# A streaming batch-norm kernel: GpSimd issues each store only after the store ahead of it has landed

## The chip, the cores and the metric

The kernel runs on one core of a Trainium2 chip. The metric is the device time of one execution in microseconds (us). Before the change three timed runs gave 2481.49, 2510.03 and 2502.17 us, so the median is 2502.17 us.

## The reference

The reference is a batch norm with given statistics over a tensor of 32 images, 256 channels and 128 x 128 pixels, all in float32. It is 537 MB in and 537 MB out.

```
eps = 1e-5
mean, var, gamma, beta: one value for each channel
return gamma * (x - mean) / np.sqrt(var + eps) + beta
```

Per channel this is one multiplication and one addition: `x * scale + shift` with `scale = gamma / sqrt(var + eps)` and `shift = beta - mean * scale`.

## The kernel before

The 256 channels are two blocks of 128, one channel per partition. An image's block is one tile of 128 partitions by 16384 floats: 8 MB, with 64 KB in each partition. There are 64 tiles (`NT = 64`), numbered i = 0 to 63, and three buffers (`NBUF = 3`), so tile i lives in buffer i % 3 and is changed in place.

Every tile passes through three steps:

- **Load.** SyncE issues the load of tile i on its own DMA queue. The first three loads are issued at once (L89 to L98; the first in two halves). From tile 3 on (L158 to L163) the load of tile i waits on the semaphore `stored[i % 3]`, which says that the store of tile i - 3 has landed, and so that the buffer is free.
- **Arithmetic.** ScalarE applies scale and shift to the whole tile in one instruction (L142), which waits for the load. VectorE takes part of the first and of the last tile (L131), and computes the scale and shift at the start.
- **Store.** GpSimd issues the stores of tiles 0 to 60 (L172), each of which waits for ScalarE (`adone`). ScalarE itself issues the last three (`NTAIL = 3`), on a queue of its own. GpSimd's stores add to `stored`, ScalarE's to `closed`.

A DMA is carried by 16 DMA engines. Each of them adds 1 to the DMA's semaphore when its share has landed, so a full landing is 16. With 128 partitions each engine carries 8 packets of 64 KB for a load and 8 for a store, and one completion packet of 4 bytes for each. The queues are q1 (SyncE's loads), q0 (GpSimd's stores) and q10 (ScalarE's last three stores).

The order is written out by hand, instruction by instruction on each engine. Nothing in it keeps GpSimd from issuing the store of tile i + 1 while the store of tile i is still under way. The loop that the change touches is the one at L165 to L174: it makes ScalarE's instruction of a tile and then the store of that tile.

Of the kernel before, what the change touches and what calls it, by code (L numbers as in the profile page):

```python
# [8 lines left out]
NBUF = 3  # L9
PAD = 936  # L10
NHEAD = 3
NTAIL = 3
# [5 lines left out]
def kernel(  # L18
# [18 lines left out]
    NT = N * NCB  # L37
# [25 lines left out]
    stored = [tc.alloc_semaphore(f"stored{s}") for s in range(NBUF)]  # L63
# [9 lines left out]
    with tc.tile_critical():  # L73
# [26 lines left out]
        def landed(i):  # L100
            if i < NHEAD:
                return first[i], 16
            s = i % NBUF
            before = 1 if s < NHEAD else 0
            return loaded[s], 16 * (i // NBUF + 1 - before)
# [34 lines left out]
        def scalar_part(i, first_col):  # L140
            t, cb = bufs[i % NBUF], i % NCB
            return nc.scalar.activation(  # L142
                out=t[:, first_col:],
                in_=t[:, first_col:],
                func=mybir.ActivationFunctionType.Identity,
                bias=shift_t[:, cb : cb + 1],
                scale=scale_t[:, cb : cb + 1],
            ).then_inc(adone, 1)


        def share(i):
            return VHEAD if i == 0 else VLAST if i == last else 0
# [12 lines left out]
        for i in range(NT):  # L165
            eng = nc.gpsimd if i < NT - NTAIL else nc.scalar
            packet = {"single_packet": True} if i < NT - NTAIL else {}
            written = (stored if i < NT - NTAIL else closed)[i % NBUF]
            scalar_part(i, share(i))._wait_ge(*landed(i))
            if i in (0, last):  # L170
                eng.wait_ge(vdone, 1 if i == 0 else 2)
            eng.dma_start(out=outr[i], in_=bufs[i % NBUF][:], **packet)._wait_ge(adone, i + 1).then_inc(  # L172
                written, 16
            )  # L174
# [39 lines left out]
```

## Time and profile before

| | us |
|---|---|
| median of the three timed runs | 2502.17 |
| profiled execution, its own time | 2481.47 |
| its span | 2479.7 |
| ScalarE busy | 885.6 |
| VectorE busy | 13.1 |
| GpSimd busy | 32.7 |
| one tile's arithmetic on ScalarE | 14.04 |
| step from one store's landing to the next, mean over stores 0 to 60 | 38.68 |
| first store: issue, landing on all engines | 31.00, 74.80 |
| last store of GpSimd (tile 60): issue, landing on all engines | 2346.87, 2395.83 |
| last store of all (tile 63): issue, landing on all engines | 2455.36, 2477.92 |

The profile is of one execution. Its page gives busy times for each engine, the share of time in which the 16 DMA engines moved something, the DMA queues, the time from issue to landing for each group of DMAs, and the chain of waits that ended last. Beneath the page lie the trace's records: each DMA packet with its start, duration, size and queue, and the time at which each DMA engine added its 1 to a semaphore. The landings in the table are read from these.

### The profile page before, as it was taken

The page shows a single profiled execution, that of the slowest core. Times are in us where ns is not written, and L with a number is a line of the kernel's source. Part 1 is how long each engine was busy: PE and PEld are TensorE (multiplying, and loading weights), DVE is VectorE, ACT ScalarE, POOL GpSimd, SP SyncE. Part 2 cuts the span into 40 slices and gives each one's busy share as a digit, 9 for nine tenths or more (in the row PEclk, how much of TensorE's full clock was granted, in tenths as well). Part 3 has the DMA queues.
Part 4 walks back from the last instruction along what each step waited for, and adds up shares of the span by engine and source line. Part 5 has one row for each costly group of instructions (what it writes and reads, how often), then busy time and mean ns, then how long its engine had stood idle before and what let it go on. Part 6 is the DMA issues. An engine that isn't in the chain of part 4 may idle for free.

```text
span 2479.7 us, 276 instructions
## 1 busy us (share of the span) xinstructions
DVE 13.1 (1%) x13; ACT 885.6 (36%) x66; POOL 32.7 (1%) x65
## 2 busy tenths in 40 slices
DVE  1000000000000000000000000000000000000000
ACT  2342432424424234242342433424334243342432
POOL 0000000000000000000000000000000000000000
DMA  9999999999999999999999999999999999999999
GB/s 410 437 440 426 437 440 428 434 440 432 430 440 432 430 440 433 429 440 436 427 440 436 427 440 437 426 440 437 426 440 437 426 440 438 425 440 438 425 440 406
DMA packets 18707, 1073.84 MB, mean 433 GB/s; under 512 B 2128, under 2 KB 2192, under 8 KB 2192
## 3 DMA queue, kind: packets, MB, share of 16 engines
q1 hardware_dynamic: 9488, 536.94, 50.0%
q0 software_dynamic: 8784, 511.71, 47.6%
q10 hardware_dynamic: 432, 25.17, 2.3%
q14 instruction: 3, 0.02, 0.0%
HBM read 536.94 MB, written 536.87 MB: 433 GB/s over the span
## 4 chain that ended last, share of the span: by engine, by line
another core or an unknown queue 61%; ACT 35%; DMA 2%; issue 0%; SPq 0%; DVE 0%; ACTq 0%; DVEq 0%
ACT t L142 35%; DMA t<-in_x_dram 2%; SPq L92 0%; DVE rows L90 0%; ACTq L172 0%; SPq L96 0%; DVE eps_t L108 0%; DVEq L209 0%; SPq L73 0%
## 5 line engine op out<-in xcount | busy, mean ns | idle before, releaser
L142 ACT ACTIVATE t<-t,shift_t,scale_t 128x16384 f32<-128x16384 f32 (+1 forms) x64 | 884.0, 13813 | 1554.8 <-DMA t<-in_x_dram 1554.8
L172 POOL DMA_DIRECT2D out_dram<-t x61 | 32.5, 534 | 2314.4 <-ACT t L142 2314.4
L131 DVE TENSOR_SCALAR t<-t,scale_t,shift_t 128x8192 f32<-128x8192 f32 (+1 forms) x2 | 9.6, 4812 | 2427.1 <-DMA t<-in_x_dram 2427.0
L115 ACT ACTIVATE std_t<-par,eps_t 128x2 f32<-128x2 f32 x1 | 0.3, 295 | 14.0 <-DVE par L113 14.0
L115 ACT ACT_TABLE_LOAD x1 | 1.3, 1283 | 0.9 <-SPq L73 0.9
L109 DVE STREAM_TRANSPOSE turned<-rows 32x1024 f32<-32x1024 f32 x1 | 1.2, 1233 | 11.9 <-DMA rows<-in_running_mean_dram 11.9
L90 DVE MEMSET rows<- 32x1024 f32 x1 | 0.9, 912 | 1.2 <-SPq L73 1.2
L113 DVE COPY par<-turned 32x8 f32<-32x8 f32 x4 | 0.6, 162 | 0.1
L122 DVE RECIPROCAL rstd_t<-std_t 128x2 f32<-128x2 f32 x1 | 0.2, 166 | 0.4 <-ACT std_t L115 0.4
L124 DVE TENSOR_TENSOR ms_t<-par,scale_t 128x2 f32<-128x2 f32 x1 | 0.2, 163 | 0.0
L125 DVE TENSOR_TENSOR shift_t<-par,ms_t 128x2 f32<-128x2 f32 x1 | 0.2, 161 | 0.0
L123 DVE TENSOR_TENSOR scale_t<-par,rstd_t 128x2 f32<-128x2 f32 x1 | 0.2, 160 | 0.0
L198 POOL MEMSET const-float32-0.0<- 128x1 f32 x1 | 0.1, 98 | 0.2 <-issue 0.2
L198 POOL MEMSET const-bfloat16-1.0<- 128x1 bf16 x1 | 0.1, 101 | 0.0
L198 POOL MEMSET const-float32-1.0<- 128x1 f32 x1 | 0.1, 98 | 0.0
L198 POOL MEMSET const-uint8-127<- 128x1 uint8 x1 | 0.1, 98 | 0.0
L108 DVE MEMSET eps_t<- 128x1 f32 x1 | 0.1, 59 | 0.1
## 6 DMA issues: line engine op xcount, KB each, us to landing
t<-in_x_dram SPq DMA_DIRECT2D x2, 4096.0 KB, 15.9
t<-in_x_dram SPq DMA_DIRECT2D x63, 55.3
out_dram<-t POOLq DMA_DIRECT2D x61, 46.2
out_dram<-t ACTq DMA_DIRECT2D x3, 32.2
rows<-in_running_var_dram SPq DMA_DIRECT2D x1, 16.0 KB, 11.3
rows<-in_gamma_dram SPq DMA_DIRECT2D x1, 16.0 KB, 11.1
rows<-in_beta_dram SPq DMA_DIRECT2D x1, 16.0 KB, 10.8
rows<-in_running_mean_dram SPq DMA_DIRECT2D x1, 16.0 KB, 10.7
```

The costliest lines, as they stand in the source:

```text
L90: zeroed = step(nc.vector.memset(rows[:], 0.0))
L109: step(nc.vector.transpose(out=turned[:], in_=rows[:]), fetched, 16 * NPAR)
L113: placed = step(nc.vector.tensor_copy(out=flat[q * B : (q + 1) * B], in_=blocks[:, :, q, 0]))
L115: nc.scalar.activation(out=std_t[:], in_=var_t, func=mybir.ActivationFunctionType.Sqrt, bias=eps_t[:], scale=1.0,)._wait_ge(vec, placed).t ...
L122: step(nc.vector.reciprocal(out=rstd_t[:], in_=std_t[:]), act, 1)
L123: step(nc.vector.tensor_mul(out=scale_t[:], in0=gamma_t, in1=rstd_t[:]))
L124: step(nc.vector.tensor_mul(out=ms_t[:], in0=mean_t, in1=scale_t[:]))
L125: ready = step(nc.vector.tensor_sub(out=shift_t[:], in0=beta_t, in1=ms_t[:]))
L131: return nc.vector.tensor_scalar(out=t[:, first_col:end], in0=t[:, first_col:end], scalar1=scale_t[:, cb : cb + 1], scalar2=shift_t[:, cb ...
L142: return nc.scalar.activation(out=t[:, first_col:], in_=t[:, first_col:], func=mybir.ActivationFunctionType.Identity, bias=shift_t[:, cb : ...
L172: eng.dma_start(out=outr[i], in_=bufs[i % NBUF][:], **packet)._wait_ge(adone, i + 1).then_inc(written, 16)
L198: nc = _bacc.Bacc("TRN2", target_bir_lowering=False, num_devices=1)
```

## The change

Two lines are added to the loop over tiles. For tiles 1 to 61, ahead of the tile's arithmetic and store, the engine that is to issue the store waits until the semaphore of the store before has its full 16 for that store.

```diff
         for i in range(NT):
             eng = nc.gpsimd if i < NT - NTAIL else nc.scalar
             packet = {"single_packet": True} if i < NT - NTAIL else {}
+            if i and i <= NT - NTAIL:
+                eng.wait_ge(stored[(i - 1) % NBUF], 16 * ((i - 1) // NBUF + 1))
             written = (stored if i < NT - NTAIL else closed)[i % NBUF]
             scalar_part(i, share(i))._wait_ge(*landed(i))
             if i in (0, last):
                 eng.wait_ge(vdone, 1 if i == 0 else 2)
             eng.dma_start(out=outr[i], in_=bufs[i % NBUF][:], **packet)._wait_ge(adone, i + 1).then_inc(
                 written, 16
             )
```

For tiles 1 to 60 the waiting engine is GpSimd. For tile 61 it is ScalarE, and there the wait stands ahead of tile 61's arithmetic as well, because both are ScalarE's. No DMA, no arithmetic and no buffer is added or taken away, and the loads' own waits stay as they were.

## The prediction

> **What bounds the kernel now.** I read the page from the DMA rows down, since ScalarE, the busiest engine, works only 36% of the span.
>
> ```profile
> DMA  9999999999999999999999999999999999999999
> ...
> DMA packets 18707, 1073.84 MB, mean 433 GB/s; under 512 B 2128, under 2 KB 2192, under 8 KB 2192
> ## 3 DMA queue, kind: packets, MB, share of 16 engines
> q1 hardware_dynamic: 9488, 536.94, 50.0%
> q0 software_dynamic: 8784, 511.71, 47.6%
> q10 hardware_dynamic: 432, 25.17, 2.3%
> ```
>
> The three shares add to 99.9%: the 16 DMA engines are busy for the whole span, so DMA time is the bound, and any idle time of the DMA engines is added to the end. The packet records say it more sharply. A 64 KB packet lasts 2.418 us, the starts of an engine's packets are mostly 2.414 us apart, and no engine is without a packet for more than about 1 us in all between its first and its last. A tile costs an engine 8 load and 8 store packets, 16 x 2.415 = 38.64 us; the landings of the stores are 38.68 us apart on average. The engines take a packet from q0 and one from q1 in turn.
>
> Next, the DMA issues, what SyncE's queue waits for, and the timeline of one tile:
>
> ```profile
> t<-in_x_dram SPq DMA_DIRECT2D x63, 55.3
> out_dram<-t POOLq DMA_DIRECT2D x61, 46.2
> ```
>
> ```profile
> SPq L160 <- DMA out_dram<-t: 2369.7, 61, 69.4
> ```
>
> ```profile
> 902.91 14.04 ACT L142 ACTIVATE t<-t,shift_t,scale_t 128x16384 f32<-128x16384 f32 x1 [24.59 <-DMA t<-in_x_dram]
> 917.25 0.53 POOL L172 DMA_DIRECT2D out_dram<-t  x1 [38.10 <-ACT t L142]
> 924.84 38.93 SPq L160 DMA_DIRECT2D t<-in_x_dram  x2
> 941.56 14.04 ACT L142 ACTIVATE t<-t,shift_t,scale_t 128x16384 f32<-128x16384 f32 x1 [24.61 <-DMA t<-in_x_dram]
> 955.89 0.53 POOL L172 DMA_DIRECT2D out_dram<-t  x1 [38.12 <-ACT t L142]
> ```
>
> A store needs 46.2 us and the next is issued after 38.6, so stores overlap: one is issued at 917.25, the one ahead of it lands at 924.82, which releases the load at 924.84. For 7.6 us of each tile two stores are queued. Also, the load before that one lands only at 941.5, 16.7 us after the store: when a store lands, an engine still has three to four load packets in hand. Both queues always hold something, which is why no engine stops.
>
> ```profile
> 924.80:941.50 16.70, 0.00 (x0) 0.00 (x0) 0.00 (x0) 1.00 1.01 440
> ```
>
> This window (fields before the last three: engines' busy times and the clock; then DMA share and GB/s) is the stretch between that landing and the load's: full rate.
>
> **The change part by part.** *The wait itself.* It binds: ScalarE has the next tile ready 7.6 us before the store ahead lands. Behind it on GpSimd are later stores only. The instruction costs GpSimd nothing that counts (32.7 us busy of 2479.7).
>
> *What it does to the queues.* In each tile an engine has 8 new load packets and 8 new store packets. While the store runs they alternate, so 8 stores take 7 or 8 loads along. But the next store now has to be asked for after the landing, and until it arrives the engine takes loads alone. The only row of a store arriving with none under way is the first: issue 31.00, first q0 packets at 35.2 to 38.2, so 4.2 us and up to one or two load packets. That is 9 to 10 loads per tile against 8 new ones: the three to four packets in hand are used up within about four tiles. From then on no load is left when a store lands, and the next load cannot be on its way, since its buffer is the one that the store has just freed. Load and store are then both asked for in the same moment, and the DMA engines stand still until the first load packet.
>
> *The size of that stop.* From the end of an engine's last store packet to its next load packet:
> - Completion to landing. The slowest engine's completion packet of store 0 starts at 74.46 and the landing is at 74.80: 0.34 us. The very last store has 2477.59 to 2477.92: 0.33. I take 0.34.
> - SyncE's reaction: landing 74.80, issue 74.82: 0.02 us.
> - Issue to data. The row that shows it with idle engines is the kernel's first load: issued at 0.96, first packet records from 1.96 on, first packets of 32 KB ended at 3.79 to 4.18. Such packets later take 1.21, so the work began in effect at 2.58 to 2.97, 1.6 to 2.0 us after the issue. The next store waits for the slowest engine, so I take 2.0; the lower end is 1.0, issue to first record.
>
> Together 2.36 us a tile, with a lower end of 1.36.
>
> *The store's own arrival* (4.2 us or more after the landing) is covered by the new load, whose 8 packets are 19.3 us of work; without that cover it would add 2.2 us a tile.
>
> *A stretch on arrival.* As store 0 joined, load packets at 32 to 38 us took up to 3.2 us in place of 2.42; per engine the excess is 0.3 to 1.0, mean 0.70. Once per tile this would now recur, if it belongs to a store that meets pure loads; it would not, if it belongs to the first use of q0 (that issue took 0.67 us, later ones 0.53). One row cannot tell, so I take half, 0.35, and keep 0 and 1.0 as ends.
>
> *Start and tail.* With loads still in hand after store 0, the first tiles wait for the store's arrival rather than for a load, some 2.4 us (one packet) more in sum. At tile 61 ScalarE waits for store 60 before its arithmetic; store 61 is then issued 14.4 us after that landing, beside load 63 with 19.3 us of packets, so the engines stay busy. After store 60's landing there remain 32 packets of an engine (load 63, stores 61 to 63): 77.3 + 2.0 + 0.3 = 79.6 us, against 82.1 now (2395.83 to 2477.92), where part of load 62 was still to come. The two nearly cancel: nothing.
>
> *Sum.* 2.36 + 0.35 = 2.71 us for each of 60 steps from store to store, 163 us. On the profiled execution, 2481.5 + 163 = 2644. The median of the runs shown is 20.7 above that execution and the lowest run equals it, so I add half, 10: 2655. Low: 60 x 1.36 = 82, 2563. High: 60 x (2.36 + 1.0) = 202 and 20.7 for the median, 2704, plus a few us for an engine's hiccup (0.34 us gaps occur) that the other 15 now wait for.
>
> *A rule beside the completion row.* The Trainium skill, page "DMA: Bandwidth & Descriptors", section "Anatomy of one DMA — SWDGE (gpsimd) path", puts a fixed cost of some 2.0 us on such a DMA, most of it the receipt of the write by the target memory. By it the stop would be 2.0 in place of 0.34, an estimate of 100 us more, 2755. The trace's 0.34 and 0.33 speak against it here.
>
> **The rivals.**
> 1. *Load packets in hand still cover the stop: no change, 2482 to 2502.* The place is the store's landing, the point one load packet in hand on every engine, 2.41 us against a stop of 2.36. For: today 16.7 us of loads are in hand there. Against: the 8 to 8 count; a load asked for at one landing finishes ahead of or with the store that it alternates with. It needs the store to be served more often than the load. 0.07.
> 2. *GpSimd's issue becomes the bound.* If loads stay in hand all the same while each store arrives late, a tile is completion behind one load packet 2.41 + 0.36 + 4.2 + 15 packets 36.2 = 43.2, up to 4.6 more than now: 60 x 4.6 = 276, 2758 to 2780. Against: loads would run ahead and run out. 0.04.
> 3. *A slow receipt that is hidden now.* Today a load packet runs between an engine's last store packet (ended 72.05 on the slowest) and its completion packet (74.46), so up to 2.41 us of receipt could be hidden. With none left to run there it would show: 2.71 + 2.41 = 5.12 a tile, 307, 2790 to 2810. Against: the last store, with no packet between, landed 0.33 after its last packet. The page cited above states such a receipt. 0.03.
> 4. *Faster, as fewer stores mix.* The duration of a packet would have to fall; it is 2.418 with loads alone (22.8 to 32) and with the two in turn. 0.02.
> 5. *The wait changes nothing*, or *the whole 46.2 us becomes the step* (60 x 7.5 = 450, 2930): the first is excluded by the 7.6 us, the second by the fact that 46.2 holds the wait behind the other store. Together 0.01, to slower.
>
> **How the numbers follow.** The stop forecast has 0.83, and its bounds 2563 to 2710 carry nearly all of that, so the range is 2560 to 2710. Slower by over 1% (25 us, which is what the three runs' own spread allows to be told): 0.83 + 0.04 + 0.03 + 0.01 = 0.91. Within 1%: 0.07. Faster: 0.02.
>
> **What would show it.** The GB/s row should fall from 433 to about 405 evenly from the second or third slice on, with the DMA share at 9 tenths or just under. Store issue to landing should fall from 46.2 to about 41, store issues should stand within 1 us behind SyncE's load issues, and the load's landing time should fall from 55.3 to about 38, since it waits behind no other load. GpSimd's waits should pass from ScalarE to the store's landing. Each packet should stay at 2.42 and a gap of 2 to 3 us appear on all 16 engines once a tile. I am wrong if packets lie in q1 at a landing (rival 1 or 2) or if a gap is over 4 us (rival 3).

## The result, and the profile after

The changed kernel took 2720.3 us (median of five runs, 2717.74 to 2725.26) against 2508.97 for the kernel before in five runs (2481.49 to 2513.75). The ratio is 1.0895, 95% interval 1.084 to 1.0951: slower, as forecast, but 65 us above the forecast and 10 us beyond its range. The profiled execution is the one of 2720.3 us; its span is 2718.5, 238.8 longer than before.

The page's DMA rows after the change. The first is GB/s in 40 equal slices of the span, the others are the queues with their share of 16 engines' span:

```profile
GB/s 418 415 357 386 401 398 389 401 386 401 401 386 401 386 401 401 386 401 386 401 401 386 401 386 401 400 378 409 371 417 386 386 414 376 414 385 387 408 394 401
...
q1 hardware_dynamic: 9488, 536.94, 49.4%
q0 software_dynamic: 8784, 511.71, 43.5%
q10 hardware_dynamic: 432, 25.17, 2.1%
```

The rate falls from 433 to 395 GB/s on average, evenly but for the third slice, which holds one long step (see below), and a few late ones. The shares now add to 95.0%, where they added to 99.9%: for one twentieth of the span the DMA engines have no packet. That q1's share hardly fell although the span grew says that its packets became longer.

The DMA issues (median us to landing):

```profile
t<-in_x_dram SPq DMA_DIRECT2D x63, 39.9
out_dram<-t POOLq DMA_DIRECT2D x61, 41.8
```

What GpSimd waits for (us in total, times, longest), first before the change, then after it, and then ScalarE after it:

```profile
POOL out_dram L172 <- ACT t L142: 2314.4, 61, 38.3
```

```profile
POOL out_dram L174 <- DMA out_dram<-t: 2531.2, 60, 52.7
ACT t L142 <- DMA t<-in_x_dram: 1696.5, 61, 36.5
```

A load lands 39.9 us after its issue, not 55.3: it no longer waits behind another load. GpSimd waited 2314 us for ScalarE before; now it waits 2531 us for stores to land.

One tile in the timeline, and three windows of it (start:end, length, busy times of three engines, clock, DMA share, GB/s):

```profile
932.15 14.04 ACT L142 ACTIVATE t<-t,shift_t,scale_t 128x16384 f32<-128x16384 f32 x1 [28.66 <-DMA t<-in_x_dram]
934.55 85.00 SPq L160 DMA_DIRECT2D t<-in_x_dram  x3
935.08 0.53 POOL L174 DMA_DIRECT2D out_dram<-t  x1 [42.17 <-DMA out_dram<-t]
```

```profile
934.20:935.50 1.30, 0.00 (x0) 1.30 (x1) 0.42 (x1) 1.00 0.00 0
935.50:976.60 41.10, 0.00 (x0) 12.93 (x2) 0.11 (x1) 1.00 0.98 408
976.60:977.70 1.10, 0.00 (x0) 1.10 (x1) 0.42 (x1) 1.00 0.00 0
```

ScalarE gets its tile at 932.15, so the load had landed by then and nothing is left in q1. The store lands at 934.54, SyncE asks for the load at 934.55, GpSimd for the next store at 935.08. No packet starts on any engine until after 935.5, and the same gap follows a tile later.

The packet records show how the growth divides. Over the execution a DMA engine stood without a packet for 137.1 us on average (0.6 before), and its packets were 102.9 us longer in all than at 2.42 us each (0.6 before). Standing and packets together fill the span, so their growth, 136.5 + 102.3 = 238.8 us, must be the growth of the span; what the records add is the share of each. For each of 60 steps between landings that is 2.28 us of standing and 1.70 us of longer packets, 3.98 us.

### The profile page after: what moved, and what is told of

The parts are those of the page before. It is cut to its first block, busy times and chain, and to the rows that moved or that the text cites. A ratio compares the mean times of both kernels' runs of the same rounds, so it can differ in the third digit from the quotient of the medians.

```text
span 2718.5 us, 337 instructions
## 1 busy us (share of the span) xinstructions
DVE 13.1 (0%) x13; ACT 885.6 (33%) x66; POOL 32.7 (1%) x65
## 4 chain that ended last, share of the span: by engine, by line
DMA 93%; another core or an unknown queue 2%; ACT 2%; issue 1%; SPq 0%; POOLq 0%; DVE 0%; ACTq 0%; POOL 0%; DVEq 0%
DMA out_dram<-t 93%; ACT t L142 2%; DMA t<-in_x_dram 1%; SPq L92 0%; POOLq L169 0%; DVE rows L90 0%; ACTq L174 0%; POOL out_dram L174 0%; DVE eps_t L108 0%; DVEq L211 0%; ACTq L169 0%; SPq L73 0%; POOLq L180 0%
## 6 DMA issues: line engine op xcount, KB each, us to landing
t<-in_x_dram SPq DMA_DIRECT2D x2, 4096.0 KB, 15.8
t<-in_x_dram SPq DMA_DIRECT2D x63, 39.9
```

## The experiments

The theory after the result was that of the prediction: the 16 DMA engines stop because, when a store lands, no load packet is in hand, no store is queued, and both are asked for only then. The rivals were a cost of GpSimd's way of issuing, a cost of serialised stores as such, and too few buffers. In all runs every tile is computed; `after` below means the changed kernel. Ratios are against runs of the kernel before on the same chip.

### Two stores may overlap again

```diff
-            if i and i <= NT - NTAIL:
-                eng.wait_ge(stored[(i - 1) % NBUF], 16 * ((i - 1) // NBUF + 1))
+            if i > 1 and i <= NT - NTAIL + 1:
+                eng.wait_ge(stored[(i - 2) % NBUF], 16 * ((i - 2) // NBUF + 1))
```

> GpSimd waits for the landing of the store two tiles back instead of one. Theory (the cost is the stop of all DMA engines when a store lands with no load packet in hand and no store queued): the store two back has landed some 31 us before the tile is ready, so two stores may still overlap, the wait never binds, and the time is that of the kernel before, 2481 to 2514 us, with stores landing 38.6 to 38.7 us apart. Rival (a wait of GpSimd for a store's semaphore costs something itself, whichever store it names): some part of the 4.0 us a tile stays, 2530 us or more.

Measured 2492.41 us against 2482.09, ratio 1.0023 (0.9977 to 1.0069); stores land 38.68 us apart in its trace, and GpSimd waits for ScalarE as before the change, for no landing:

```profile
POOL out_dram L174 <- ACT t L142: 2314.4, 61, 38.5
```

A wait that does not bind costs nothing that can be measured. This run does not tell whether the missing load or the missing store behind the landing costs the time; the halves below do.

### A store issued 10 us later

```diff
                 eng.wait_ge(stored[(i - 1) % NBUF], 16 * ((i - 1) // NBUF + 1))
+                if eng is nc.gpsimd:
+                    for _ in range(10):
+                        inst = nc.gpsimd.memset(pad[:], 0.0)
+                        if padded[0]:
+                            inst._wait_ge(slow, padded[0])
+                        inst.then_inc(slow, 1)
+                        padded[0] += 1
```

> As the changed kernel, but GpSimd also fills a scratch tile ten times (about 10 us) between the store's landing and the issue of the next store. Theory (the new load's 8 packets, 19.3 us of work, cover the store's arrival): the time stays within 1% of the changed kernel, 2695 to 2750 us, and store issue stands some 10 us after the load's issue. If the stretch of the second load packet belongs to the store's arrival, it moves to the packets that run then and the second one lasts 2.4 us; if it belongs to loads that start on idle engines, packets one and two stay at 3.2 and 3.4 us. Rival (GpSimd's issue is on the path): 60 x 10 = 600 us more, about 3300 us.

Measured 2718.01 us in one run. Its timeline:

```profile
929.71 0.33 SPq L162 DMA_DIRECT2D t<-in_x_dram  x1
929.81 9.30 POOL L174 MEMSET pad<- 128x936 f32 x10 [32.84 <-DMA out_dram<-t]
939.06 0.53 POOL L183 DMA_DIRECT2D out_dram<-t  x1
```

The store goes out 9.4 us after the landing instead of 0.5, and the time is that of the changed kernel: the load covers the store's arrival, and GpSimd's issue is not on the path. Where the longer packets went is read from one DMA engine's packets after a landing (us after it : duration, L from the load's queue, S from the store's). The records do not name the engine; a chain is put together from packets that start where another ends:

```
after       1.09:3.23 L  4.31:3.31 L  7.62:2.42 S 10.04:2.42 L 12.45:2.42 S
late_store  0.98:3.23 L  4.20:2.42 L  6.61:2.42 L  9.03:2.43 L 11.45:3.44 L 14.89:2.42 S
```

The first packet is long in both, by 0.67 us on average: that is the load's start on an idle engine. The other long one is no longer the second packet but the last load packet ahead of the first store packet, by 0.95 us on average after the change and 1.26 here. It belongs to the store's arrival. That the two totals agree to 2 us has some luck in it: the median step is 42.58 us here against 42.29, but one long step of the changed kernel (53.27 us, see below) is missing.

### A store issued 23 us later

The edit is the same with `range(25)`.

> As the run with ten fills ahead of GpSimd's store, with 25 fills, 23.2 us by the 0.93 us of one fill there. Theory (a load's 8 packets end some 21 us after the landing and cover a store that arrives before that): the store now arrives about 27 us after the landing, the engines stand a second time for 5 to 7 us, the stretch at the arrival goes because no load runs then, and the tile is about 47 us: 2950 to 3050 us. Rival (a late store costs nothing, or all of its lateness): 2718 us, or 23 x 60 = 1390 us more.

Measured 2824.95 us in one run: the estimate was too high, though the second stop and the missing stretch are there. Four windows of one tile:

```profile
920.40:921.40 1.00, 0.00 (x0) 0.00 (x0) 0.83 (x1) 1.00 0.00 0
921.40:941.80 20.40, 0.00 (x0) 0.00 (x0) 19.13 (x23) 1.00 0.98 411
941.80:944.90 3.10, 0.00 (x0) 2.52 (x1) 2.48 (x4) 1.00 0.00 0
944.90:964.90 20.00, 0.00 (x0) 11.52 (x1) 0.00 (x0) 1.00 0.97 419
```

Loads alone, then 3.1 us without a packet, then stores alone. GpSimd issued the store at 943.86 and the packets start at 945.0, 1.1 to 1.2 us later, not 4.2. So a store of GpSimd reaches an idle engine about as soon as a load does (1.0 us and more); on an engine at work with loads it waits for the packet that runs and for one more. A tile takes 44.4 us here, and no packet ahead of a store is long: with no load running there is no stretch.

### ScalarE issues the stores

```diff
-            eng = nc.gpsimd if i < NT - NTAIL else nc.scalar
-            packet = {"single_packet": True} if i < NT - NTAIL else {}
-            if i and i <= NT - NTAIL:
-                eng.wait_ge(stored[(i - 1) % NBUF], 16 * ((i - 1) // NBUF + 1))
+            eng = nc.scalar
+            packet = {}
             written = (stored if i < NT - NTAIL else closed)[i % NBUF]
             scalar_part(i, share(i))._wait_ge(*landed(i))
+            if i and i <= NT - NTAIL:
+                eng.wait_ge(stored[(i - 1) % NBUF], 16 * ((i - 1) // NBUF + 1))
```

> ScalarE issues all stores on its own queue, each after the landing of the one ahead (the wait stands behind the tile's arithmetic); GpSimd issues none. Theory (the stop is common to any queue, since load and store are asked for at the same landing): 2.0 us of standing and 0.7 us of start remain, 2640 to 2680 us if the stretch at the store's arrival is a matter of GpSimd's queue, 2690 to 2730 us if any store brings it. Rival (the cost is GpSimd's way of issuing): 2481 to 2520 us.

Measured 3221.24 us in one run, far above every expectation. Timeline and one window:

```profile
930.54 51.39 SPq L160 DMA_DIRECT2D t<-in_x_dram  x2
930.60 0.34 ACTq L174 DMA_DIRECT2D out_dram<-t  x1
```

```profile
930.60:981.60 51.00, 0.00 (x0) 14.04 (x1) 0.00 (x0) 1.00 0.89 329
```

Load and store are issued 0.06 us apart, and a tile takes 51 us: an engine stands 357 us in the whole run and its packets are 384 us longer, about half of them over 2.6 us, all through the tile. The shares of one store land 5.7 us apart at the median. Two runs look for the cause. The first takes the wait away, with all stores still ScalarE's:

> ScalarE issues all stores, each right behind its tile's arithmetic, with no wait for the store ahead: the control for the run with serialised stores on ScalarE's queue, whose tile took 51 us with packets of up to 3.4 us. If ScalarE's queue beside SyncE's is slow by itself, stretched packets appear here too and the time is 2600 us or more; if the stretching needs load and store to arrive together on idle engines, packets are 2.42 us and the time is 2480 to 2520 us.

Measured 2503.66 us, packets 15.5 us longer in all: ScalarE's queue beside SyncE's is not slow by itself. The second keeps the wait but lets eight fills by GpSimd pass between the landing and ScalarE's issue:

```diff
             if i and i <= NT - NTAIL:
-                eng.wait_ge(stored[(i - 1) % NBUF], 16 * ((i - 1) // NBUF + 1))
+                for n in range(8):
+                    inst = nc.gpsimd.memset(pad[:], 0.0)
+                    if n == 0:
+                        inst._wait_ge(stored[(i - 1) % NBUF], 16 * ((i - 1) // NBUF + 1))
...
+                eng.wait_ge(slow, padded[0])
```

> As the run with serialised stores on ScalarE's queue (51 us a tile), but between the landing and the store's issue GpSimd fills a scratch tile eight times, some 7.4 us, and ScalarE waits for that; the load goes out at once. If the stretched packets of that run came from load and store reaching idle engines together, the tile falls to 41 to 43 us and the time to 2630 to 2740 us. If they come from two hardware queues that restart at each landing, whatever their order, the tile stays at 50 us or more, 3150 us or more.

Measured 2710.0 us, with this timeline:

```profile
927.13 43.33 SPq L162 DMA_DIRECT2D t<-in_x_dram  x2
927.16 7.42 POOL L174 MEMSET pad<- 128x936 f32 x8 [35.22 <-DMA out_dram<-t]
934.67 0.34 ACTq L184 DMA_DIRECT2D out_dram<-t  x1
```

A later store makes the kernel 511 us faster. On these two queues the disorder of the serialised run needs load and store to reach idle engines together. With a few load packets ahead, ScalarE's store costs what GpSimd's costs, and the packet ahead of the store is as long here (3.3 to 4.1 us in the tile shown): the stretch is not GpSimd's. Why packets stay long for a whole tile after a common start is not settled.

### Halves: a load in hand at the landing

```diff
-            inst = nc.sync.dma_start(out=bufs[s][:], in_=xr[i])
-            if i >= NBUF:
-                inst._wait_ge(stored[s], 16 * (i // NBUF))
-            inst.then_inc(loaded[s], 16)
+            for half, sem in ((left, stored), (right, stored2)):
+                inst = nc.sync.dma_start(out=bufs[s][:, half], in_=xr[i][:, half])
+                if i >= NBUF:
+                    inst._wait_ge(sem[s], 16 * (i // NBUF))
+                inst.then_inc(loaded[s], 16)
...
                 eng.wait_ge(stored[(i - 1) % NBUF], 16 * ((i - 1) // NBUF + 1))
+                eng.wait_ge(stored2[(i - 1) % NBUF], 16 * ((i - 1) // NBUF + 1))
...
+            for half, sem in ((left, stored), (right, stored2)):
+                eng.dma_start(out=outr[i][:, half], in_=bufs[i % NBUF][:, half], **packet)._wait_ge(
+                    adone, i + 1
+                ).then_inc(sem[i % NBUF], 16)
```

> Loads and GpSimd's stores move a tile as two halves of 4 MB. Both halves of a store still wait until both halves of the store ahead have landed; a half's load waits only for that half's store, so it is asked for while the other half is still being stored. Theory (the cost is that load and next store are asked for at the same landing, with no load packet in hand): a half load is now in hand when the store lands, so the standing of about 2 us and the start of 0.8 us go and only the stretch at the store's arrival, about 1 us, is left: 2500 to 2620 us. Rival (serialising GpSimd's stores costs by itself): 2690 us or more.

Measured 2564.01 us against 2498.34, ratio 1.0273 (1.0196 to 1.035). The control has the halves without the wait:

> The same halves without the wait for the store ahead: the control for the run before. Both theories: the DMA engines stay full, 2480 to 2520 us.

Measured 2510.39 us in one run. The DMA issues of the run with the wait:

```profile
t<-in_x_dram SPq DMA_DIRECT2D x124, 4096.0 KB, 21.9
out_dram<-t POOLq DMA_DIRECT2D x122, 4096.0 KB, 35.2
```

GpSimd's stores are serialised as strictly as in the changed kernel, tile by tile. Yet an engine now stands only 6.4 us in the whole run instead of 137.1: when the second half of a store lands, 15.8 of the 16 engines are in the middle of a load packet on average. The longer packets remain, 68.5 us against 16.6 in the control, 0.87 a tile. This is the theory's central test: with load packets in hand the standing goes and the stretch stays, although the next store is still asked for only after the landing.

### Half-size tiles in six buffers

```diff
-NBUF = 3
+NBUF = 6
-NTAIL = 3
+NTAIL = 6
...
-    HW = H * W
-    NT = N * NCB
+    HW = H * W // 2
+    NT = N * NCB * 2
```

> Tiles of half the size (4 MB, 128 of them) in six buffers that take the same space, with the wait for the store ahead (the last six stores are ScalarE's, without it). Theory (each landing costs the same, since loads run ahead and then every buffer is loaded and waits, so the next load can again be asked for only at the landing): 3.7 to 4.0 us at each of 121 landings, 2930 to 2990 us. Rival (three buffers are too few; with six some load is always in hand): 2480 to 2620 us.

Measured 2863.09 us, ratio 1.1476 (1.1334 to 1.1619). The control:

> The same six half-size buffers without the wait: the control. Both theories: 2480 to 2520 us.

Measured 2487.65 us in one run. With the wait, load and store are again asked for half a microsecond apart at the landing:

```profile
911.88 45.30 SPq L162 DMA_DIRECT2D t<-in_x_dram  x3
912.40 0.53 POOL L176 DMA_DIRECT2D out_dram<-t  x1 [22.01 <-DMA out_dram<-t]
```

More buffers in the same space do not help: a landing costs (2861.1 - 2485.9) / 121 = 3.1 us by the spans of the two profiled executions, though a tile has half the bytes, so the cost goes with the number of landings. It is less than the 3.7 to 4.0 expected: by the packet records 1.8 us of standing and 1.4 us of longer packets, which at 32 KB are shorter by themselves.

### The wait at every fourth tile

```diff
-            if i and i <= NT - NTAIL:
+            if i and i % 4 == 0 and i <= NT - NTAIL:
```

> The wait stands only at every fourth tile, 15 waits instead of 61. Theory: load packets in hand (three to four an engine when a store lands) cover one late store, and the following free stores restore them, so the engines stand still hardly at all; what is left is the stretch of two load packets when a store arrives, about 1 us a wait: 2485 to 2530 us. Rival (each serialised landing costs its 4.0 us on its own, whatever lies in hand): 15 x 4.0 = 60 us, 2545 to 2575 us.

Measured 2597.09 us, ratio 1.0426 (1.0359 to 1.0494). Both sides missed: 15 waits cost 115 us by the medians and 112 by the spans of the profiled executions, over 7 each, more than a wait in the changed kernel. Windows around the landing at 516.0, for which GpSimd waits:

```profile
468.00:507.00 39.00, 0.00 (x0) 14.04 (x1) 0.00 (x0) 1.00 1.03 447
507.00:516.00 9.00, 0.00 (x0) 0.00 (x0) 0.00 (x0) 1.00 0.22 95
516.00:517.00 1.00, 0.00 (x0) 0.00 (x0) 0.46 (x1) 1.00 0.76 262
```

For 9 us ahead of the landing most engines have nothing to do; the semaphore's records show the first engine's share landing 16.3 us before the last one's. At the first two waited landings it is 3.1 and 2.3 us, at the later ones mostly 14 to 16. The spread is 3.1 us at the median in the kernel before and 0.78 in the changed kernel, where all engines restart together at each tile. With three free tiles between two waits, one to three of the 16 engines come to lag. The others end 5 to 7 us ahead of the waited landing, and "landed on all engines" means waiting for the few. What makes them fall behind stays open. A run in which GpSimd waits for one engine's share of the store ahead instead of all 16 (2680 to 2725 us expected, 2480 to 2600 if the wait for the last engine is what costs) gave no result, because such a wait can pass before the store has landed; so a wait for fewer engines is untested.

## Why the forecast was wrong in size

- **What bounds the kernel: right.** The growth lies in the DMA engines, 136.5 us of standing and 102.3 of longer packets, and GpSimd's issue is off the path: 9.4 us after the landing instead of 0.5, it leaves the time as it is.
- **Loads run out, and load and store are asked for at the same landing: right.** Nothing is in q1 at the landing, GpSimd's issue is 0.53 us behind SyncE's, and the first step, with loads still in hand, is 43.29 us against the 43.2 worked out. Halves put a load in hand and the standing goes.
- **The size of the stop: too small, and with no end above it.** It was 2.36 us a tile, which was also its highest value. The measured counterpart is 2.28 us of standing and 0.67 of the load's first packet, 2.95. The single terms were right for the slowest engine: 0.36 us from its last packet's end to the landing, and first load packets 1.0 us and more after the issue. What was left out is that every other engine waits for the slowest one. On average an engine ends its last packet 1.02 us ahead of the landing (the long step below left aside), and its first load packet starts 1.2 us after it. The steps of 43 us among the typical 42.3 are, after the first, those in which the shares of a store land 1.5 to 2.0 us apart.
- **The stretch on arrival: off by most.** Half of 0.70 us was taken because one row could not tell a first use of the queue from a store that meets running loads. Taking the store later moved the long packet along with it, giving it no load to meet removed it, and ScalarE's queue shows it too. It recurs at every landing, 0.95 us in the changed kernel; with a few more long packets it is 1.70 - 0.67 = 1.03 against 0.35. So the sign that each packet stays at 2.42 us did not hold. Stop and stretch fall short by 0.59 + 0.68 = 1.27 us a step, 76 us: 2644 + 76 = 2720, the measured time, as it must be when all standing and all packets are counted. The range allowed the stretch up to 1.0; it was the stop, 0.59 us a step or 35 us over its upper end, that carried the time past it.
- **One step of 53.27 us**, from the second store to the third, 11 us over the typical one, is within these averages and was not foreseen. Its packets are up to 4.6 us long, as in the run where load and store start together, and the shares of the store that ends it land 8.1 us apart. The cause is open.
- **The store's arrival: right that it is covered, wrong in its 4.2 us.** Into an idle engine it is 1.1 to 1.2; the 4.2 held the packet that ran and one more.
- **Start and tail: right.** From the landing of GpSimd's last store to the last landing there are 81 us, 79.6 worked out, and no gain or loss that counts.
- **The rivals.** Load packets in hand did not cover the stop. A slow receipt did not show: 0.36 us on the slowest engine with nothing between its last packet and the landing. The Trainium skill, page "DMA: Bandwidth & Descriptors", section "Anatomy of one DMA — SWDGE (gpsimd) path", states some 2 us, most of it the receipt; this trace does not agree, and that the time by its rule came out near is by other terms. The added 10 us for the runs' median was not needed, since the five runs lie around the profiled one.

## What to carry to other kernels

Where DMA is the bound, count what each queue still holds at the moment a completion is waited for: if the same landing releases the next load and the next store, every landing costs the whole restart, completion, issue, first packet, and the spread over the engines. Keep one transfer queued behind the one that runs, or split transfers so that a part of the next load is released ahead of the landing; more buffers in the same space do not help. A single odd row in a trace, such as two long packets at a first store, deserves its full price when the change repeats just that situation; here even the full 0.70 us would have been short of 1.03.

## What the runs showed of the hardware that was not expected

- When a store reaches engines busy with loads alone, the last load packet ahead of it is longer: 3.4 to 3.7 us on average over three runs in place of 2.42, from GpSimd's queue and from ScalarE's.
- A load of SyncE and a store of ScalarE that reach idle engines 0.06 us apart keep packets long for a whole tile: 51 us a tile, against 42.5 when the store is issued 7.5 us later.
- Engines that restart together at every tile land their shares of a store 0.78 us apart at the median in the changed kernel, but 5.7 us apart where load and store start together; with a wait at every fourth tile the first share lands mostly 14 to 16 us ahead of the last, because one to three engines lag.
